# ConvFFN gate and up projections as one 2x2x2 Strassen block product on one Trainium2 core

## The chip, the cores and the metric

The kernel runs on one core of one Trainium2 chip. A core has TensorE (PE: matrix products out of SBUF into PSUM, with a weight load for each), VectorE (DVE), ScalarE (ACT), GpSimd (POOL) and SyncE (SP, whose queue issues the loads and stores). The metric is the device time of one execution in microseconds (us), the median of the runs.

## What is computed

One inference step of a one-layer hybrid decoder, D_MODEL 1024, 2048 prompt tokens and 8 x 4 sample tokens, all in fp32. The change touches the gated ConvFFN with D_FF = 3072, the last part of the layer:

```python
def causal_dwconv(x, prev, w, b):
    K = w.shape[0]
    T = x.shape[1]
    xp = jnp.concatenate([prev.astype(x.dtype), x], axis=1)
    y = b + sum(w[k] * xp[:, k:k + T] for k in range(K))
    return y, xp[:, T:]
...
    n3 = rmsnorm(x, p['g_ffn'])
    g, ffn_state = causal_dwconv(n3 @ p['w_ffn_gate'], ffn_prev, p['w_ffn_conv'], p['b_ffn_conv'])
    x = x + (jax.nn.gelu(g) * (n3 @ p['w_ffn_up'])) @ p['w_ffn_down']
    return x, (buf_k, buf_v, conv_state, h_last, ffn_state)
```

Ahead of it stand the input projection with a gated recurrence and windowed attention, the output projection and a cross-attention to 256 memory tokens; behind it the final RMSNorm.

## The kernel before

Channels and features lie on the 128 partitions, tokens along the free dimension. Each fp32 operand is split into a high and a low part (`split`, L75: ACT copies the high part at L78, DVE or POOL subtracts to get the low part at L82), and each product is three matmuls: high by high, high by low, low by high (`mm3`, L120).

The phases run in program order; a scheduler orders each engine's queue by priority and dependence, so phases overlap at their borders. Phases 0 to 2 take up to about 1100 us. Phase 3 is the ConvFFN. It takes the tokens in three blocks (SB3, L37: 704, 688, and 656 with the 32 sample tokens). For each block it reads the residual x back from DRAM (x2d), normalises it (`p3_norm`, L595) and keeps the split result n3 as 16 tiles, 8 channel tiles of 128 with a high and a low one each, out of 28 tile names that go round, so that 12 of a next block's tiles are others than this block's. The norm of block 0 is issued at a high priority (N3_PRIO), that of the next block after feature tile 20 of the 24; the scheduler puts those of its operations whose tiles are free much further ahead.

For each feature tile f of 128 (`gate_up`, L1149): the gate's and the up's 96 matmuls (8 channel tiles, 2 token halves, 3 products, 2 projections), into PSUM tiles named pg; ACT copies the gate to gb (L1166); DVE does the three convolution taps into gc (a tensor_scalar at L1176 and two scalar_tensor_tensor at L1178); ACT does the gelu (L1179); DVE multiplies with the up product, read out of PSUM (L1183); ACT and POOL split the result into ah and al. After every second f, `down` (L1197) does the 96 matmuls of the two f before it into PSUM tiles pd (8 output tiles), and DVE adds each to the accumulator acc (L1208). The product down(f-2, f-1) stands in the program behind gate_up(f), at a block's border behind the next block's first feature.

Weights come through `weights` (L107), in units of 128 x 1024 in the order of use, two units ahead: a DMA into wr (four buffers), the high part wh by ACT, the low part wl by POOL (three buffers each). A gate, an up or a down tile of a feature is one unit.

## Time and profile before

| | |
|---|---|
| median of 3 runs | 2786.28 us (2780.19 to 2796.98) |
| span of the profiled execution | 2790.0 us |
| busy over the span | PE 96%, DVE 50%, ACT 36%, POOL 44% |
| chain that ended last | PE 75%, DVE 3%, DMA 2%, POOL 1% |
| phase 3 | about 1100 us to the end |
| DMA | 276.91 MB, mean 99 GB/s |

Busy time counts an engine's instructions that compute; register, branch, semaphore and DMA-issuing ones are left out. The chain that ended last is followed back from the last instruction, at each step to what released it. Shares over the whole span mix phases with different limits, so phase 3 is read by itself in the rows below.

### The profile page before, as it was taken

What the parts mean: (1) busy time and instruction counts of PE and PEld (TensorE: products, weight loads), DVE (VectorE), ACT (ScalarE), POOL (GpSimd) and SP (SyncE); (2) the same over time, 40 slices, a digit from 0 to 9 for tenths busy, and PEclk for the clock granted to TensorE, in tenths of its full rate; (3) what the DMA queues carried; (4) which work ended last, traced back from release to release, by engine and by line L of the source; (5) the groups of instructions that cost most, each with busy time, mean ns of one, the idle gap of its engine ahead of it and who ended that gap; (6) DMA issues with size and microseconds to landing.
All of it is one profiled execution on the core that took longest, in us unless ns stands there. A gap on an engine that the chain in (4) does not pass through costs nothing.

```text
span 2790.0 us, 39744 instructions
## 1 busy us (share of the span) xinstructions
PE 2688.0 (96%) x16085; PEld 2531.3 (91%) x16085; DVE 1399.4 (50%) x2135; ACT 1011.5 (36%) x1749; POOL 1219.3 (44%) x802
## 2 busy tenths in 40 slices
PE   7998988998999998999999999999999999999997
PEld 6786867986998887999999999999999999999997
DVE  7568687758563545533333345333333443333435
ACT  5474736465453544322222223222222232222222
POOL 3444544314635364543434345444344454444343
PEclk8999999999999999999999999999999999999998
DMA  6342412244435344311121234212212241112121
GB/s 225 118 133 72 135 65 96 83 147 149 137 112 202 111 150 139 119 69 68 68 69 68 68 98 146 76 68 77 69 69 70 75 147 71 69 68 76 62 76 52
DMA packets 117463, 276.91 MB, mean 99 GB/s; under 512 B 19940, under 2 KB 40676, under 8 KB 117280
## 3 DMA queue, kind: packets, MB, share of 16 engines
q1 hardware_dynamic: 117280, 274.37, 28.9%
q8 instruction: 126, 2.06, 0.3%
q14 instruction: 57, 0.47, 0.1%
HBM read 244.13 MB, written 30.20 MB: 98 GB/s over the span
## 4 chain that ended last, share of the span: by engine, by line
PE 75%; DVE 3%; DMA 2%; POOL 1%; issue 1%; ACT 1%; SPq 0%; POOLq 0%; DVEq 0%; ACTq 0%
PE pg L125 37%; PE pd L125 19%; PE po L125 7%; PE pq L125 3%; PE pmo L125 3%; PE pin L125 2%; PE mpo L125 1%; DMA x<-x2d 1%; PE msc L125 1%; DMA yraw<-ymix 1%; PE mtp L1011 1%; DVE x L604 1%; PE spo L1127 0%; PE sst L1088 0%; PE pt L125 0%
## 5 line engine op out<-in xcount | busy, mean ns | idle before, releaser
L82 POOL TENSOR_TENSOR wl<-wr,wh 128x1024 fp32r<-128x1024 f32 x341 | 824.4, 2423 | 1313.0 <-ACT wh L78 1247.6
L125 PE MATMUL pg<-n,wh 128*128 128x344 f32 (+1 forms) x4608 | 919.0, 321 | 0.6 <-POOL n L82 0.3
L125 PEld LDWEIGHTS pg<-n,wh 128*128 128x128 f32 x4608 | 765.2, 188 | 1.2 <-POOL n L82 0.6
L78 ACT ACTIVATE wh<-wr 128x1024 fp32r<-128x1024 f32 x326 | 341.4, 1057 | 1100.7 <-PE pd L125 403.8
L125 PE MATMUL pg<-n,wl 128*128 128x344 f32 (+1 forms) x2304 | 552.1, 321 | 0.0
L1176 DVE TENSOR_SCALAR gc<-gb,pp 128x704 f32<-128x704 f32 (+1 forms) x72 | 146.7, 2037 | 542.2 <-ACT gb L1166 356.3
L125 PEld LDWEIGHTS pg<-n,wl 128*128 128x128 f32 x2304 | 398.9, 188 | 0.1
L1208 DVE TENSOR_TENSOR acc<-pd,acc 128x688 f32<-128x688 f32 (+1 forms) x280 | 246.4, 880 | 278.6 <-PE pd L125 273.5
L125 PE MATMUL pd<-ah,wh 128*128 128x344 f32 (+1 forms) x1120 | 270.5, 323 | 9.5 <-DVE acc L1208 9.5
L125 PE MATMUL pd<-al,wh 128*128 128x344 f32 (+1 forms) x1120 | 269.7, 322 | 0.0
L125 PE MATMUL pd<-ah,wl 128*128 128x344 f32 (+1 forms) x1120 | 269.5, 322 | 0.0
L125 PEld LDWEIGHTS pd<-ah,wh 128*128 128x128 f32 x1120 | 195.7, 190 | 10.4 <-DVE acc L1208 10.3
L125 PE MATMUL pin<-n1h,wh 128*128 128x512 f32 (+1 forms) x560 | 188.5, 361 | 9.4 <-DVE ql L82 9.4
L125 PEld LDWEIGHTS pd<-al,wh 128*128 128x128 f32 x1120 | 196.0, 190 | 0.0
L125 PEld LDWEIGHTS pd<-ah,wl 128*128 128x128 f32 x1120 | 195.6, 190 | 0.0
L125 PE MATMUL pin<-n1l,wh 128*128 128x512 f32 (+1 forms) x560 | 186.7, 358 | 2.1 <-DVE n1l L82 2.1
L125 PE MATMUL pin<-n1h,wl 128*128 128x512 f32 (+1 forms) x560 | 185.3, 356 | 0.0
L1179 ACT ACTIVATE gc<-gc 128x704 f32<-128x704 f32 (+1 forms) x72 | 56.8, 788 | 301.5 <-DVE gc L1178 301.5
L1178 DVE SCALAR_TENSOR_TENSOR gc<-gb,pp,gc 128x704 f32<-128x704 f32 (+1 forms) x144 | 141.9, 985 | 4.9
L125 PEld LDWEIGHTS pin<-n1h,wh 128*128 128x128 f32 x560 | 103.3, 193 | 25.8 <-DVE ql L82 9.7
L82 POOL TENSOR_TENSOR al<-at,ah 128x688 fp32r<-128x688 f32 (+1 forms) x72 | 124.1, 1724 | 5.7 <-ACT ah L78 5.7
L125 PEld LDWEIGHTS pin<-n1l,wh 128*128 128x128 f32 x560 | 102.8, 193 | 18.2 <-DVE n1l L82 4.1
(313 smaller groups left out, 3923.9 us busy)
## 6 DMA issues: line engine op xcount, KB each, us to landing
wr<-in_w_gate_dram SPq DMA_DIRECT2D x72, 512.0 KB, 3.2
wr<-in_w_up_dram SPq DMA_DIRECT2D x72, 512.0 KB, 3.2
wr<-in_w_down_dram SPq DMA_DIRECT2D x72, 512.0 KB, 3.2
wr<-in_w_in_dram SPq DMA_DIRECT2D x56, 512.0 KB, 3.2
...
wr<-in_w_out_dram SPq DMA_DIRECT2D x32, 512.0 KB, 3.3
...
wr<-in_w_mem_q_dram SPq DMA_DIRECT2D x16, 512.0 KB, 4.5
```

The lines of the kernel that those rows point to most:

```text
L78: nc.scalar.activation(hi, src, AF.Copy)
L82: e.tensor_tensor(out=lo, in0=src, in1=hi.bitcast(F), op=OP.subtract)
L125: nc.tensor.matmul(o, w[a], xs, start=first and n == 0, stop=last and n == 2)
L604: nc.vector.scalar_tensor_tensor(x, x, self.col(G_FFN, k), rt, op0=OP.mult, op1=OP.mult)
L1011: nc.tensor.transpose(tp[:, i], P[:, i, c * 128:(c + 1) * 128], K.ident)
L1176: nc.vector.tensor_scalar(gc, gb[:, 2:2 + NW], K.col(C_FW, 48 + f), K.col(C_FB, f), op0=OP.mult, op1=OP.add)
L1178: nc.vector.scalar_tensor_tensor(gc, gb[:, k:k + NW], K.col(C_FW, 24 * k + f), gc, op0=OP.mult, op1=OP.add)
L1179: nc.scalar.activation(gc, gc, AF.Gelu_apprx_tanh)
L1208: nc.vector.tensor_tensor(out=v, in0=pd[:, :, 0:H], in1=v, op=OP.add)
```

## The change

The gate and the up product of a feature tile are taken as one product of 2 x 2 blocks, A x B. A has the gate's first and second half of the channels (a11, a12) in its first row and the up's (a21, a22) in its second. B has the first and second half of the channels as rows and the two token halves of the block as columns (b11 to b22). Winograd's form of Strassen's product does this with seven block products and sums: of A, s1 = a21 + a22, s2 = s1 - a11, s3 = a11 - a21, s4 = a12 - s2; of B, t1 = b12 - b11, t2 = b22 - t1, t3 = b22 - b12, t4 = b21 - t2. ORDER and BUDDY list the pairs.

- Weights: `piece_stream` and `piece` take the place of `weights` in phase 3. Pieces are 128 x 512 (4 channel tiles), four ahead, six buffers for each of the high and low parts, three for sums, four raw buffers as before. DVE makes four sums `ws` per feature, ACT and POOL split seven pieces per feature and four per down product.
- Activations: `p3_norm` makes seven operands for each of four channel tiles, 28 pairs of high and low tiles of half a block's width, with four DVE subtractions for each; low parts alternate between POOL and DVE. The tiles n3_0 to n3_55 have one buffer each, and the next block's norm is issued after f = 23, no longer after 20. The x tiles have three buffers, and not two.
- Features: `gate_up` does 84 matmuls, accumulates in four PSUM halves X, Y, Z, V, and forms the two outputs by a copy u and adds u2, u4 and those into gb and up out of PSUM. The first convolution tap is done by ACT. up and gc have one buffer, and up x gc reads SBUF alone.
- Blocks are now 696, 692 and 660 with the 32 sample tokens.

```diff
-SB3 = [(0, 704, False), (704, 688, False), (1392, 656, True)]
+SB3 = [(0, 696, False), (696, 692, False), (1388, 660, True)]
+ORDER = ("a11", "s2", "s1", "s3", "a12", "s4", "a22")
+BUDDY = ("b11", "t2", "t1", "t3", "b21", "b22", "t4")
...
-            self.wspl = pool(name="wspl", bufs=3)
...
+    def piece_stream(self):
+
+        nc, I = self.nc, self.I
+
+        def load(src):
+            raw = self.wraw.tile([128, 1024], F, name="wr", tag="wr")
+            nc.sync.dma_start(raw, src)
+            return raw[:, 0:512], raw[:, 512:1024]
+
+        def sums(x, y, op):
+            t = self.wsum.tile([128, 512], F, name="ws", tag="ws")
+            nc.vector.tensor_tensor(out=t, in0=x, in1=y, op=op)
+            return t
+
+        def halves(src):
+            hi = self.wpc.tile([128, 512], R, name="ph", tag="ph")
+            lo = self.wpc.tile([128, 512], R, name="pl", tag="pl")
+            self.split(src, hi, lo, "act", "pool")
+            return hi, lo
+
+        def paired(f):
+            a11, a12 = load(I["w_gate"][f])
+            a21, a22 = load(I["w_up"][f])
+            yield halves(a11)
+            s1 = sums(a21, a22, OP.add)
+            s2 = sums(s1, a11, OP.subtract)
+            yield halves(s2)
+            yield halves(s1)
+            yield halves(sums(a11, a21, OP.subtract))
+            yield halves(a12)
+            yield halves(sums(a12, s2, OP.subtract))
+            yield halves(a22)
+
+        def plain(c):
+            raws = [load(I["w_down"][c * CH + i]) for i in range(CH)]
+            for h in range(2):
+                for i in range(CH):
+                    yield halves(raws[i][h])
+
+        for s in range(3):
+            for f in range(NF):
+                yield from paired(f)
+                if f % CH == 0 and (f or s):
+                    yield from plain((f // CH - 1) % (NF // CH))
+        yield from plain(NF // CH - 1)
...
+    def piece(self, ahead=4):
+        while len(self.pq) <= ahead:
+            p = next(self.pieces, None)
+            if p is None:
+                break
+            self.pq.append(p)
+        return self.pq.pop(0)
...
-                    if f == 20 and s < 2:
+                    if f == NF - 1 and s < 2:
...
-        x = self.xs.tile([128, W], F, name="x3", tag="x", bufs=2)
+        x = self.xs.tile([128, W], F, name="x3", tag="x", bufs=3)
...
-    def n3_tile(self, W):
-        i = self.n3i % 28
-        self.n3i += 1
-        return (self.n3a if i < 13 else self.n3b).tile([128, W], R, name=f"n3_{i}")
-
     def p3_norm(self, s):
         nc, q1 = self.nc, self.xs
         t0, w, smp = SB3[s]
         W = w + (NS if smp else 0)
+        H = W // 2
         rt = q1.tile([128, W], F, name="rt3")
         self.p3_dma(rt, self.r3d, t0, W)
-        nh, nl = [], []
-        for k in range(KT):
-            x = self.p3_load(s, k)
-            nc.vector.scalar_tensor_tensor(x, x, self.col(G_FFN, k), rt, op0=OP.mult, op1=OP.mult)
-            h, l = self.n3_tile(W), self.n3_tile(W)
-            self.split(x, h, l, "act", "pool" if k % 2 else "dve")
-            nh.append(h)
-            nl.append(l)
-        return nh, nl
+        ops, n = {}, 0
+        for k in range(KT // 2):
+            xs = []
+            for kk in (k, k + KT // 2):
+                x = self.p3_load(s, kk)
+                nc.vector.scalar_tensor_tensor(x, x, self.col(G_FFN, kk), rt, op0=OP.mult, op1=OP.mult)
+                xs.append(x)
+            b11, b12, b21, b22 = xs[0][:, 0:H], xs[0][:, H:W], xs[1][:, 0:H], xs[1][:, H:W]
+            v = dict(b11=b11, b21=b21, b22=b22)
+            for nm, x, y in (("t1", b12, b11), ("t2", b22, "t1"), ("t3", b22, b12), ("t4", b21, "t2")):
+                v[nm] = q1.tile([128, H], F, name="t3", tag="t", bufs=4)
+                nc.vector.tensor_tensor(out=v[nm], in0=x, in1=v[y] if isinstance(y, str) else y, op=OP.subtract)
+            for nm in BUDDY:
+                hl = []
+                for e in "hl":
+                    hl.append((self.n3a if n < 26 else self.n3b).tile([128, H], R, name=f"n3_{n}"))
+                    n += 1
+                self.split(v[nm], hl[0], hl[1], "act", "pool" if n % 4 else "dve")
+                ops[nm, k] = hl
+        return ops
...
-        K, nc, q1, q2, I, s = self.K, self.K.nc, self.K.q1, self.K.q2, self.K.I, self.s
-        w, W, H, NW, smp, subs = self.w, self.W, self.H, self.NW, self.smp, self.subs
-        res = []
-        for nm in ("w_gate", "w_up"):
-            wt = K.weights(I[nm][f])
-            ps = K.psum([128, 2, 512], "pg", "pg")
-            outs = [ps[:, e, 0:H] for e in range(2)]
-            K.proj(wt, self.nh, self.nl, outs, subs, KT)
-            res.append(ps)
-            if nm == "w_gate":
-                gb = q2.tile([128, NW + 2], F, name="gb")
-                if s == 0:
-                    nc.gpsimd.memset(gb[:, 0:2], 0.0)
...
-                    nc.gpsimd.tensor_copy(gb[:, 0:2], K.p3c[s - 1][:, f])
...
-                    nc.scalar.activation(gb[:, 2:2 + W].rearrange("p (a b) -> p a b", a=2), ps[:, :, 0:H], AF.Copy)
...
-                nc.gpsimd.tensor_copy(self.carry[:, f], gb[:, w:w + 2])
-                gc = q2.tile([128, NW], F, name="gc")
-                nc.vector.tensor_scalar(gc, gb[:, 2:2 + NW], K.col(C_FW, 48 + f), K.col(C_FB, f), op0=OP.mult, op1=OP.add)
-                for k in range(2):
-                    nc.vector.scalar_tensor_tensor(gc, gb[:, k:k + NW], K.col(C_FW, 24 * k + f), gc, op0=OP.mult, op1=OP.add)
-                nc.scalar.activation(gc, gc, AF.Gelu_apprx_tanh)
-        pu = res[1]
-        at = q1.tile([128, W], F, name="at", bufs=1)
-        if not smp:
-            nc.vector.tensor_tensor(out=at.rearrange("p (a b) -> p a b", a=2), in0=pu[:, :, 0:H],
...
+        K, nc, q1, q2, s = self.K, self.K.nc, self.K.q1, self.K.q2, self.s
+        w, W, H, NW, smp = self.w, self.W, self.H, self.NW, self.smp
+        xy = K.psum([128, 2, 512], "pg", "pg")
+        zw = K.psum([128, 2, 512], "pg", "pg")
+        X, Y, Z, V = (t[:, e, 0:H] for t in (xy, zw) for e in range(2))
+        add = lambda o, p, t: nc.vector.tensor_tensor(out=o, in0=p, in1=t, op=OP.add)
+        tmp = lambda nm: q2.tile([128, H], F, name=nm, tag="hv", bufs=3)
+
+        def product(i, out, first):
+            hi, lo = K.piece()
+            for k in range(KT // 2):
+                ws = [t[:, k * 128:(k + 1) * 128] for t in (hi, lo)]
+                K.mm3([out], ws, [[t] for t in self.ops[BUDDY[i], k]], first and k == 0, k == KT // 2 - 1, not first)
+
+        gb = q2.tile([128, NW + 2], F, name="gb")
+        if s == 0:
+            nc.gpsimd.memset(gb[:, 0:2], 0.0)
         else:
-            nc.vector.tensor_tensor(out=at[:, 0:H], in0=pu[:, 0, 0:H], in1=gc[:, 0:H], op=OP.mult)
...
+            nc.gpsimd.tensor_copy(gb[:, 0:2], K.p3c[s - 1][:, f])
+        up = q1.tile([128, W], F, name="up")
+        product(0, X, True)
+        u = tmp("u")
+        nc.scalar.activation(u, X, AF.Copy)
+        product(1, Y, True)
+        u2 = tmp("u2")
+        add(u2, Y, u)
+        product(2, Z, True)
+        u4 = tmp("u4")
+        add(u4, Z, u2)
+        product(3, V, True)
+        add(up[:, H:W], V, u4)
+        product(4, X, False)
+        nc.scalar.activation(gb[:, 2:2 + H], X, AF.Copy)
+        product(5, Z, False)
+        n = w - H
+        add(gb[:, 2 + H:2 + w], Z[:, 0:n], u2[:, 0:n])
+        if smp:
+            gv = gb[:, 2 + w:2 + w + 6 * NB].rearrange("p (b e) -> p b e", e=6)
+            nc.gpsimd.tensor_copy(gv[:, :, 0:2], K.fst[:, f])
+            bt = lambda t: t[:, n:H].rearrange("p (b t) -> p b t", t=NT)
+            add(gv[:, :, 2:6], bt(Z), bt(u2))
...
+        product(6, V, False)
+        add(up[:, 0:H], V, u2)
+        gc = q1.tile([128, NW], F, name="gc")
+        nc.scalar.activation(gc, gb[:, 2:2 + NW], AF.Identity, scale=K.col(C_FW, 48 + f), bias=K.col(C_FB, f))
+        for k in range(2):
+            nc.vector.scalar_tensor_tensor(gc, gb[:, k:k + NW], K.col(C_FW, 24 * k + f), gc, op0=OP.mult, op1=OP.add)
+        nc.scalar.activation(gc, gc, AF.Gelu_apprx_tanh)
+        nc.vector.tensor_tensor(out=up[:, 0:w], in0=up[:, 0:w], in1=gc[:, 0:w], op=OP.mult)
...
-        wts = [K.weights(K.I["w_down"][ch * CH + i]) for i in range(CH)]
         for m in range(KT):
+            if m % 4 == 0:
+                wts = [K.piece() for i in range(CH)]
             pd = K.psum([128, 2, 512], "pd", "pd")
             outs = [pd[:, e, 0:H] for e in range(2)]
             for i in range(CH):
-                ws = [t[:, m * 128:(m + 1) * 128] for t in wts[i]]
+                ws = [t[:, m % 4 * 128:(m % 4 + 1) * 128] for t in wts[i]]
```

Three places of DVE's queue show what stands where. First, block 0 in steady state. Before, the rows of a feature pair are two feature paths and the accumulator adds:

```order
L1176 TENSOR_SCALAR gc<-gb,pp 128x704
L1178 SCALAR_TENSOR_TENSOR gc<-gb,pp,gc 128x704 x2
L1183 TENSOR_TENSOR at<-pg,gc 128x704
L1176 TENSOR_SCALAR gc<-gb,pp 128x704
L1178 SCALAR_TENSOR_TENSOR gc<-gb,pp,gc 128x704 x2
L1183 TENSOR_TENSOR at<-pg,gc 128x704
L1208 TENSOR_TENSOR acc<-pd,acc 128x704 x8
```

Now, in the feature ahead of a down product (the u rows are the adds u2 and u4, ws are the weight sums, of the next feature from the first ws on):

```order
L1207 TENSOR_TENSOR u_13722<-pg,u 128x348
L1207 TENSOR_TENSOR u_13740<-pg,u_13722 128x348
L538 TENSOR_TENSOR ws<-wr 128x512
L538 TENSOR_TENSOR ws<-ws,wr 128x512
L538 TENSOR_TENSOR ws<-wr 128x512
L1207 TENSOR_TENSOR up<-pg,u_13740 128x348
L1207 TENSOR_TENSOR gb<-pg,u_13722 128x348
L1250 SCALAR_TENSOR_TENSOR gc<-gb,pp,gc 128x696 x2
L1207 TENSOR_TENSOR up<-pg,u_13722 128x348
L1274 TENSOR_TENSOR acc<-pd,acc 128x696
L1252 TENSOR_TENSOR up<-up,gc 128x696
L1274 TENSOR_TENSOR acc<-pd,acc 128x696 x2
```

Three of the next feature's four weight sums stand between the feature's add u4 and its add up, the fourth among the accumulator adds; the tap at L1176 is gone. Second, phase 2's end, of the cross-attention of the last tokens. Before, rows of block 0's norm (L604, L82) stood among its softmax:

```order
L996 SCALAR_TENSOR_TENSOR nm<-mx,rcs 128x2
L82 TENSOR_TENSOR ptl<-mtp,pth 128x512
L604 SCALAR_TENSOR_TENSOR x_10619<-x_10619,pp,rt_10568 128x704
L996 SCALAR_TENSOR_TENSOR nm<-mx,rcs 128x2
L82 TENSOR_TENSOR ptl<-mtp,pth 128x512
L604 SCALAR_TENSOR_TENSOR x_10627<-x_10627,pp,rt_10568 128x704
L1000 RECIPROCAL mrs<-mrs 128x4
L1002 TENSOR_SCALAR P<-P,mrs 128x256 x4
```

Now the norm (L647, L653) begins behind the last residual add of phase 2 (x_7, L1095):

```order
L1095 TENSOR_TENSOR x_7_9932<-pmo,x_7_9932 128x512
L538 TENSOR_TENSOR ws<-wr,ws 128x512
L538 TENSOR_TENSOR ws<-wr 128x512
L538 TENSOR_TENSOR ws<-ws,wr 128x512
L647 SCALAR_TENSOR_TENSOR x_10566<-x_10566,pp,rt_10563 128x696
L171 RECIPROCAL rc<-rc 128x4
L653 TENSOR_TENSOR t_10574<-x_10566 128x348
L647 SCALAR_TENSOR_TENSOR x_10570<-x_10570,pp,rt_10563 128x696
L188 COPY rt<-pr 128x512
L653 TENSOR_TENSOR t_10576<-x_10570,t_10574 128x348
```

All eight normalising products of block 0 moved behind phase 2's adds, with three weight sums ahead of them. Third, the border of blocks 0 and 1. Before, rows of block 2's norm (whose tiles came free with block 0's) stood there among down's adds:

```order
L82 TENSOR_TENSOR n_13_19202<-x_19196,n_12_19201 128x688
L1208 TENSOR_TENSOR acc<-pd,acc 128x704 x2
L604 SCALAR_TENSOR_TENSOR x_19214<-x_19214,pp,rt_19156 128x688
L1208 TENSOR_TENSOR acc<-pd,acc 128x704
L604 SCALAR_TENSOR_TENSOR x_19223<-x_19223,pp,rt_19156 128x688
L1208 TENSOR_TENSOR acc<-pd,acc 128x704 x4
L1176 TENSOR_SCALAR gc<-gb,pp 128x688
L1178 SCALAR_TENSOR_TENSOR gc<-gb,pp,gc 128x688 x2
L1183 TENSOR_TENSOR at<-pg,gc 128x688
L181 RECIPROCAL rc<-rc 128x5
```

Now, during feature 23 of block 0 (n are low parts of the next block's operands, t their differences, u, up and gb the feature's adds):

```order
L84 TENSOR_TENSOR n_7_15873<-t_15856,n_6_15872 128x346
L653 TENSOR_TENSOR t_15902<-x_15892,t_15898 128x346
L1207 TENSOR_TENSOR up<-pg,u_15750 128x348
L538 TENSOR_TENSOR ws<-wr,ws 128x512
L647 SCALAR_TENSOR_TENSOR x_15932<-x_15932,pp,rt_15841 128x692
L84 TENSOR_TENSOR n_11_15881<-x_15848,n_10_15880 128x346
L1207 TENSOR_TENSOR gb<-pg,u_15732 128x348
L653 TENSOR_TENSOR t_15940<-x_15932 128x346
L1250 SCALAR_TENSOR_TENSOR gc<-gb,pp,gc 128x696
L84 TENSOR_TENSOR n_27_15929<-t_15902,n_26_15928 128x346
L1207 TENSOR_TENSOR up<-pg,u_15732 128x348
```

The norm of block 1 stands in between the adds of feature 23 itself, and goes on behind them.

## Rows read from the trace of the kernel before

L is the line in the kernel before; `wr` is a raw weight, names are the program's tiles, out<-in.

**Rows 1.** The page's part 4: the chain that ended last, by line
```profile
PE pg L125 37%; PE pd L125 19%; PE po L125 7%; PE pq L125 3%; PE pmo L125 3%; PE pin L125 2%; PE mpo L125 1%; DMA x<-x2d 1%; PE msc L125 1%; DMA yraw<-ymix 1%; PE mtp L1011 1%; DVE x L604 1%; PE spo L1127 0%; PE sst L1088 0%; PE pt L125 0%
```

**Rows 2.** Busy us of each engine in 100 us of block 0
```profile
core 0: us, PE busy (x) PEld busy (x) DVE busy (x) ACT busy (x) POOL busy (x), PEclk, DMA share, GB/s
1400.00:1500.00 100.00, 100.00 (x621) 100.00 (x620) 37.19 (x36) 23.08 (x26) 37.99 (x25) 1.00 0.19 64
```

**Rows 3.** TensorE's waits, 1110 to 2700: us in total, times, longest
```profile
PE pd L125 <- DVE acc L1208: 9.5, 3, 5.2
```

**Rows 4.** The chain in order of time: start us, us, what
```profile
1173.68 31.04 PE pg L125 x192
...
2650.21 30.12 PE pg L125 x192
```

**Rows 5.** Groups of DVE, POOL, ACT by shape: xcount | busy, mean
```profile
L1208 DVE TENSOR_TENSOR acc<-pd,acc 128x688 f32<-128x688 f32 x184 | 160.9, 875 | 181.8 <-PE pd L125 176.7 <-DMA acc<-x2d 5.1
...
L1178 DVE SCALAR_TENSOR_TENSOR gc<-gb,pp,gc 128x704 f32<-128x704 f32 x96 | 94.2, 981 | 3.3
...
L1186 DVE TENSOR_TENSOR at<-pg,gc 128x344 f32<-128x344 f32 x24 | 12.4, 516 | 46.8 <-PE pg L125 45.8 <-ACT gc L1179 0.9
...
L1043 DVE TENSOR_TENSOR x<-pmo,x 128x512 f32<-128x512 f32 x8 | 5.4, 690 | 11.7 <-PE pmo L125 11.7
...
L1057 POOL TENSOR_TENSOR ssum<-ssum,sq 128x512 f32<-128x512 f32 x7 | 9.0, 1291 | 0.2
...
L82 POOL TENSOR_TENSOR al<-at,ah 128x688 fp32r<-128x688 f32 x48 | 81.0, 1688 | 5.7 <-ACT ah L78 5.7
...
L1049 ACT ACTIVATE sq<-x 128x512 f32<-128x512 f32 x10 | 6.3, 631 | 6.9 <-DVE x L1043 4.4 <-DVE x1s L1053 2.4
...
L1168 ACT ACTIVATE gb<-pg 128x344 f32<-128x344 f32 x24 | 10.5, 438 | 0.0
```

**Rows 6.** Timeline of DVE, then POOL: start us, us, engine, line
```profile
1653.08 0.86 DVE L82 TENSOR_TENSOR n<-x,n 128x688 fp32r<-128x688 f32 x1
...
1656.06 0.94 DVE L604 SCALAR_TENSOR_TENSOR x<-x,pp,rt 128x688 f32<-128x688 f32 x1 [1.26 <-DMA x<-x2d]
...
1657.78 2.22 DVE L604 SCALAR_TENSOR_TENSOR x<-x,pp,rt 128x688 f32<-128x688 f32 x1
1659.91 2.37 DVE L82 TENSOR_TENSOR n<-x,n 128x688 fp32r<-128x688 f32 x1
...
1656.65 2.61 POOL L82 TENSOR_TENSOR wl<-wr,wh 128x1024 fp32r<-128x1024 f32 x1 [1.53 <-DMA x<-x2d]
1659.22 2.33 POOL L82 TENSOR_TENSOR al<-at,ah 128x704 fp32r<-128x704 f32 x1
1661.52 2.31 POOL L82 TENSOR_TENSOR n<-x,n 128x688 fp32r<-128x688 f32 x1
```

**Rows 7.** The page's part 6, weight load: KB, us to landing
```profile
wr<-in_w_gate_dram SPq DMA_DIRECT2D x72, 512.0 KB, 3.2
```

**Rows 8.** Stretches around three TensorE waits; the matmuls that waited
```profile
1160.00:1166.00 6.00, 6.00 (x25) 6.00 (x24) 0.93 (x2) 0.00 (x0) 2.35 (x2) 0.57 0.26 87
1680.00:1685.00 5.00, 5.00 (x22) 5.00 (x22) 2.02 (x3) 1.58 (x2) 3.81 (x3) 0.61 0.33 84
1690.00:1695.00 5.00, 5.00 (x33) 5.00 (x32) 2.64 (x3) 3.44 (x5) 4.84 (x4) 1.00 0.00 0
...
1159.08 0.96 PE L125 MATMUL pd<-ah,wh 128*128 128x352 f32 x2 [3.49 <-DVE acc L1208]
...
1678.94 0.95 PE L125 MATMUL pd<-ah,wh 128*128 128x352 f32 x2 [5.22 <-DVE acc L1208]
...
1688.02 0.59 PE L125 MATMUL pd<-ah,wh 128*128 128x352 f32 x2 [0.76 <-DVE acc L1208]
```

**Rows 9.** Timeline of DVE, two rows ahead of the FFN
```profile
1060.89 0.95 DVE L604 SCALAR_TENSOR_TENSOR x<-x,pp,rt 128x704 f32<-128x704 f32 x1 [0.80 <-DMA x<-x2d]
...
1099.90 0.69 DVE L1043 TENSOR_TENSOR x<-pmo,x 128x512 f32<-128x512 f32 x1 [2.07 <-PE pmo L125]
```

More of the change, by code (lines that the diff above doesn't have):

```diff
@@ L118, in weights, with mm3 @@
         return self.wq.pop(0)
-    def mm3(self, outs, w, x, first, last):
+    def mm3(self, outs, w, x, first, last, more=False):
         nc = self.nc
@@ L124, in mm3 @@
             for o, xs in zip(outs, x[b]):
-                nc.tensor.matmul(o, w[a], xs, start=first and n == 0, stop=last and n == 2)
+                nc.tensor.matmul(o, w[a], xs, start=first and n == 0, stop=last and n == 2, skip_group_check=more)
     def proj(self, w, xh, xl, outs, subs, nk):
@@ L562, in phase3 @@
                     if len(pend) == CH:
[L563 removed]
+                        (sb if f else last).down(pend)
                         pend = []
@@ L1220, in tail @@
         nc.sync.dma_start(K.O["s_ffn_conv"], K.sfo)
-        wts = [K.weights(K.I["w_down"][NF - CH + i]) for i in range(CH)]
+        wts = [K.piece() for i in range(2 * CH)]
         warm = K.q2.tile([128, 1], F, name="warm")
```

62 lines of the change are left out of this document (23 added, 39 removed).

## The prediction

> **What bounds the kernel now.** I began with the chain that ended last [rows 1]: the FFN's two products on TensorE (PE), pg (gate and up) and pd (down), carry 37 and 19% of the span in it. Then a stretch of the FFN phase, which runs from about 1100 us to the end [rows 2]: in steady state PE is busy all of 100 us at full granted clock, DVE 37%, POOL 38%. The list of PE's waits says the same from the other side [rows 3]: from 1110 to 2700 us pd waited three times, 9.5 us in all. So a matmul removed there is time removed, if the new feeding work keeps up. The chain in order of time prices the matmuls [rows 4]: 192 of 352 columns take 31.04 us (161.7 ns each), 192 of 344 take 30.12 (156.9). One pair of features (2 f and the down product after them, 288 matmuls) costs 46.56 or 45.17 us, by the three blocks 45.6 in the mean (288 x 161.7 or 156.9).
>
> **What is removed.** Seven block products of 4 x 3 matmuls take the place of eight, so a feature needs 84 matmuls and not 96: 72 x 12 = 864 fewer. The new halves of 348, 346 and 346 columns lie between the two priced sizes, 158.5 ns in the mean. Removed: 864 x 0.1585 = **-137 us**, and a pair without a wait would take 264 x 0.1585 = 41.8 us. The order of instructions does have these counts, so "it does not do what it says" is no case here.
>
> By the Trainium skill, "TensorE: Matmul & The Clock Gate", section "Back-to-back issue gap", a warm matmul takes its columns over 2.4 GHz plus about 2.5 ns, an estimate of 147.5 ns at 348 columns and so 127 us removed. The rows here are 14 ns above that rate at 352 and 344 columns, and the sum goes by the rows.
>
> **What is added in every pair of features.** DVE gets eight weight sums `ws` of 512 columns, adds of half width out of PSUM (u2, u4, two up, one gb) in each feature, and a product up x gc that now has both inputs in SBUF; its first tap goes to ACT. POOL makes eighteen low parts of 512 columns in place of six of 1024 columns. Durations [rows 5]: low part 1.29 (a POOL operation of the same kind and size), `al` 1.69, sum about 0.69 (a 512-column add), half-width add 0.52, tap 0.98, up x gc about 0.88 (between 0.86 and 0.94 of [rows 6]), ACT's high part of 512 columns 0.63, half-width copy 0.44.
>
> PE no longer has a cheap supply. Two things decide: how the supply loop is closed, and what DVE and POOL do to each other.
>
> *DVE against POOL.* [rows 6] shows the same kinds of operation together. DVE's normalising product, 0.94 us at 1656.06, took 2.22 at 1657.78, when it came while POOL made a low part; it ended at 1660.00, 0.78 behind POOL's end. POOL's next one, 1.69 in the mean [rows 5], took 2.33; DVE's next subtraction, 0.86 at 1653.08, took 2.37; POOL's next took 2.31. They pass each other in turn, one whole instruction each. The accumulator adds with one input in PSUM do not take part: 875 ns in the mean of 184, though POOL is busy 38% of the time [rows 2, 5]. So `ws`, the taps and up x gc take turns with POOL and the adds from PSUM don't. Demand on that turn per pair: POOL 18 x 1.29 + 2 x 1.69 = 26.6, DVE 8 x 0.69 + 4 x 0.98 + 2 x 0.88 = 11.2, together 37.8 of 41.8 us. It would just fit if it could be spread at will.
>
> The Trainium skill, "SBUF — State Buffer", section "Who interferes with whom", gives this as a rule against such a change: a DVE instruction with two SBUF inputs and a GpSimd instruction that reads SBUF exclude each other, and the later one waits out the whole of the first. The rows agree (2.22 us for 0.94). If the rule were soft, and the two shared, the case "no turns" below would be the forecast.
>
> *The loop.* Call B the feature ahead of a down product, C the next one. The raw weights have four buffers, so the load of C's up weights waits until the low part of B's seventh piece is made; that piece needs the buffer of B's first piece, which frees when PE ends product 1 of B. In DVE's queue the three sums of C that need this load stand ahead of the add up[H:] of B, and PE's sixth product of B waits for that add, since it writes the same PSUM tile. From the end of product 1 of B: copy u 0.44, high part 0.63, low part 1.29 (ended at 2.43 with what the hops take, some 0.03 each), issue to landing 3.2 [rows 7] with another hop: landed at 5.70. POOL meanwhile goes on with `al` (to 4.12), D0 (5.41), D1 (6.70). The first sum, 0.29 us too late for D1, runs 6.70 to 7.39; D2 to 8.68, second sum to 9.37, D3 to 10.66, third to 11.35, add to 11.87. PE has four products until then, 48 x 0.1585 = 7.6 us. It waits **4.3 us**; if the first sum slips in ahead of D1, **3.0**; if nobody takes turns, 5.70 + 3 x 0.69 + 0.52 = 8.3, **0.7**. I take 3.0: the margin is 0.29 us, and anything that holds POOL back puts the sum first.
>
> *The clock.* The two long gaps of before tell what such a wait brings after it [rows 8]. After 3.49 us the granted clock was 0.57 in 1160 to 1166, and 25 matmuls ran in 6 us, where 5 us hold 33 at clock 1.00 (1690 to 1695): 2.2 us lost. After 5.22 us it was 0.61 in 1680 to 1685, 22 in place of 33: 1.7 us lost. That is mostly the lower of its two levels, 1.2 GHz. After the wait of 0.76 us at 1688 it stood at 1.00. So 3.0 us of waiting costs 5.0. The other waits of a pair (the fourth sum stands ahead of the gb add in the feature without a down product; PE's next product reads a PSUM tile that ACT still copies) come to 0.6, at most 1.2.
>
> Stall per pair 3.0 + 2.0 + 0.6 = **5.6 us** (1.3 without turns, 7.7 with the late sum). Steady pairs are 36 less one at the start of each block: 33 x 5.6 = **+185 us** (43 to 254). A pair then lasts 47.4 us against 45.6.
>
> **Start of the FFN.** Before, block 0's eight normalising products ran inside phase 2 (the last at 1060.89), and PE could go from phase 2's products to pg [rows 9]; counted back from 1173.68 [rows 4] by the 384 matmuls done, 384 x 0.1617, it started in effect at 1111.6. Now all of block 0's operands come behind phase 2's last add (1099.90 + 0.69): 8 x 0.94 + 16 x 0.52 + 14 x 0.52 = 23 us on DVE, 14 x 0.92 (the line through POOL's 512 and 688 columns in [rows 5]) = 13 on POOL. In turn that is 36, to about 1136, and product 1 needs the last channel tile of it: **+24 us**. If DVE's 23 alone count, +12; with waits for the three x buffers, +40.
>
> **Two block seams.** Before, most of a next block's norm ran a block ahead, into tiles that were partly doubled; the losses were the 6 us of [rows 3] that came behind the 3.49. Now all operands are single, so they can be overwritten only while feature 23 runs its products, and down(22,23) stands behind the next block's first feature. Norm (18 on DVE, 13 on POOL) and the weight pieces (16 us) make about 47 us in turn over 13.3 us of PE work: a gap of 34; with DVE and POOL side by side 13. I take 27 each, 54 less 6 us that seams cost before: **+48** (20 to 62).
>
> **Sum.** -137 + 185 + 24 + 48 = +120 on the profiled 2790.0 us: 2910. The median of the runs is 3.7 us below the span, so 2906.
>
> **Rivals.**
> - *PE stays the bound* (faster). The four pieces of lead absorb the loop, because a hand schedule puts waits in line that a queue hides. Stall under 1 us a pair: -137 + 30 + 12 + 20 = -75, **2711 us**. For it: PE's share of [rows 2], and the turn's demand of 37.8 is under 41.8. Against: lead in pieces does not move the load, which hangs on the buffer of product 1. It decides if PE's stall stays under 2 us a pair, for (137 - 24 - 48)/33 = 2.0 is the point of no gain or loss.
> - *No turns*, the load alone late: 33 x 1.3 = 43: -137 + 43 + 24 + 48 = -22, **2764**. Against it are the two DVE rows over 2 us of [rows 6].
> - *Late sum each time*: 254 in place of 185, **2975**; it belongs to the forecast's side.
>
> **Chances.** Forecast with the late sum 0.70, PE bound 0.17, no turns 0.13. A measurement of this kernel tells about 0.5% (14 us) from no change. The first gives 0.68 slower and 0.02 same; the second is faster; the third, with its start and seams free, 0.05 faster, 0.05 same, 0.03 slower. Faster 0.22, same 0.07, slower 0.71. The range leaves out a tenth at each end: 2700 (a little below PE bound) to 2985 (late sum, with part of the worse seams).
>
> **What will show it.** Matmuls of the FFN fall by 864. Right: PE's waits list pg behind DVE's up, ws or POOL's low parts, once a pair and over 2.5 us; `ws` means well above 0.69 us; granted clock of a steady 100 us below 0.97; a pair every 47 to 50 us; gaps of 20 us or more at the start and the two seams. Wrong: a pair of 42 to 43.5 us at clock 1.00 (PE bound), or long PE waits with `ws` at 0.7 (no turns). If the pairs are right and the start is not, the last x reloads are the term to look at.

## The result, and the profile after

The changed kernel takes 2981.14 us (median of 4 runs, 2978.46 to 2989.74), the kernel before 2786.98 beside it (4 runs, 2780.19 to 2796.98): 1.070 times as long, 95% interval 1.067 to 1.073. That is on the side that was forecast and inside its range (2700 to 2985), though by 4 us only, and 75 us above the 2906 forecast. The profiled execution's span is 2980.4 us, 190.4 more than before.

The page's first part, of the changed kernel: busy time, share of the span, instructions.

```profile
PE 2669.9 (90%) x15221; PEld 2438.5 (82%) x15221; DVE 1829.8 (61%) x2789; ACT 1279.3 (43%) x2337; POOL 1616.3 (54%) x1264
```

PE has the 864 matmuls fewer (16085 before), and is busy 90% of a longer span, where it was 96%. The same 100 us as in [rows 2], and 4 us behind one of its waits, with the same columns:

```profile
1400.00:1500.00 100.00, 91.50 (x545) 87.44 (x545) 53.16 (x65) 36.01 (x59) 57.69 (x49) 0.98 0.21 68
...
1424.00:1428.00 4.00, 3.71 (x14) 3.71 (x15) 0.30 (x2) 0.17 (x1) 0.94 (x1) 0.57 0.83 255
```

PE is busy 91.5 us where it was 100, and DVE and POOL are only half busy: no engine is full. What PE waits for, over the whole span (the view of [rows 3]):

```profile
PE pg L121 <- DVE up L1207: 79.1, 62, 2.6
PE pd L121 <- DVE acc L1274: 57.3, 36, 3.2
PE pg L121 <- ACT n L80: 21.0, 6, 4.4
...
PE pg L121 <- DVE n L84: 13.9, 3, 6.2
```

The first two come mostly from the steady pairs, the two of n from the norm at the start and the seams. One pair in the timeline (start us, us, engine, line, and in brackets the idle time before with its releaser), PE first, then DVE, then POOL:

```profile
1421.83 0.32 PE L121 MATMUL pg<-n,pl 128*128 128x348 f32 x1
1424.29 0.95 PE L121 MATMUL pg<-n,ph 128*128 128x348 f32 x2 [2.14 <-DVE up L1207]
...
1420.02 1.33 DVE L538 TENSOR_TENSOR ws<-wr 128x512 f32<-128x512 f32 x1 [1.21 <-DMA wr<-in_w_up_dram]
1421.44 0.69 DVE L538 TENSOR_TENSOR ws<-ws,wr 128x512 f32<-128x512 f32 x1
1422.05 1.76 DVE L538 TENSOR_TENSOR ws<-wr 128x512 f32<-128x512 f32 x1
1423.73 0.51 DVE L1207 TENSOR_TENSOR up<-pg,u 128x348 f32<-128x348 f32 x1
...
1438.40 1.75 DVE L538 TENSOR_TENSOR ws<-wr,ws 128x512 f32<-128x512 f32 x1 [1.85 <-POOL pl L84]
1440.07 0.87 DVE L1274 TENSOR_TENSOR acc<-pd,acc 128x696 f32<-128x696 f32 x1
...
1418.25 2.55 POOL L84 TENSOR_TENSOR pl<-wr,ph 128x512 fp32r<-128x512 f32 x2
1421.70 3.24 POOL L84 TENSOR_TENSOR pl<-wr,ph 128x512 fp32r<-128x512 f32 x2 [0.90 <-ACT ph L80]
```

The forecast loop is there. DVE stands idle until the up weights land at about 1420.0; its first sum takes 1.33 us beside POOL's low part, the second, while POOL waits for ACT, 0.69, the third 1.76. Only then comes the add that PE waits for: 2.14 us listed as idle. The second wait was not in the forecast. The fourth sum waits 1.85 us for one of POOL's low parts, because the sums have three buffers, and then takes 1.75; behind it in DVE's queue stands the accumulator add at 1440.07, on which the down product waits. The groups of 1250 to 1600 us by shape (count | busy us, mean ns | idle before) answer to [rows 5]:

```profile
L538 DVE TENSOR_TENSOR ws<-wr 128x512 f32<-128x512 f32 x29 | 32.1, 1108 | 17.7 <-POOL pl L84 9.5 <-DMA wr<-in_w_up_dram 8.2
...
L538 DVE TENSOR_TENSOR ws<-wr,ws 128x512 f32<-128x512 f32 x14 | 24.6, 1759 | 22.8 <-POOL pl L84 22.8
...
L1207 DVE TENSOR_TENSOR up<-pg,u 128x348 f32<-128x348 f32 x28 | 14.4, 513 | 16.2 <-PE pg L121 16.2
```

Sums of two raw halves last 1.1 us in the mean and the fourth sum 1.76, where a 512-column add had taken 0.69; the second sum, which in block 0 meets POOL waiting for ACT, keeps 0.69; adds out of PSUM stay at 0.51. From the end of one down product to the next, 28 steady pairs took 1366.5 us (10 from 1204.18 to 1690.94, 9 from 1869.69, 9 from 2487.47): 48.8 us a pair, 7.0 above the 41.84 of its matmuls.

### The profile page after: what moved, and what is told of

Same layout as the page of the kernel before. It is cut to its first block, busy times and chain, and to the rows that moved or that the text cites. A ratio compares the mean times of both kernels' runs of the same rounds, so it can differ in the third digit from the quotient of the medians.

```text
span 2980.4 us, 41018 instructions
## 1 busy us (share of the span) xinstructions
PE 2669.9 (90%) x15221; PEld 2438.5 (82%) x15221; DVE 1829.8 (61%) x2789; ACT 1279.3 (43%) x2337; POOL 1616.3 (54%) x1264
## 5 line engine op out<-in xcount | busy, mean ns | idle before, releaser
L121 PE MATMUL pg<-n,ph 128*128 128x346 f32 (+1 forms) x4032 | 1012.4, 337 | 145.6 <-DVE up L1207 79.1
L121 PEld LDWEIGHTS pg<-n,ph 128*128 128x128 f32 x4032 | 712.7, 195 | 206.5 <-DVE up L1207 99.0
L84 POOL TENSOR_TENSOR pl<-wr,ph 128x512 fp32r<-128x512 f32 x360 | 500.1, 1399 | 451.9 <-ACT ph L80 430.6
L121 PE MATMUL pg<-n,pl 128*128 128x346 f32 (+1 forms) x2016 | 647.6, 329 | 1.0 <-POOL pl L84 1.0
L84 POOL TENSOR_TENSOR wl<-wr,wh 128x1024 fp32r<-128x1024 f32 x125 | 306.4, 2453 | 550.0 <-ACT wh L80 454.9
L84 POOL TENSOR_TENSOR pl<-ws,ph 128x512 fp32r<-128x512 f32 x288 | 379.8, 1329 | 177.6 <-ACT ph L80 177.4
L121 PEld LDWEIGHTS pg<-n,pl 128*128 128x128 f32 x2016 | 392.8, 196 | 1.4 <-POOL pl L84 1.3
L121 PE MATMUL pd<-ah,ph 128*128 128x346 f32 (+1 forms) x1120 | 282.4, 331 | 62.0 <-DVE acc L1274 57.3
L121 PE MATMUL pd<-ah,pl 128*128 128x346 f32 (+1 forms) x1120 | 276.8, 325 | 2.4 <-POOL pl L84 2.4
L121 PE MATMUL pd<-al,ph 128*128 128x346 f32 (+1 forms) x1120 | 274.9, 327 | 2.4 <-POOL al L84 2.4
```

What stands on the lines that cost most here:

```text
L84: e.tensor_tensor(out=lo, in0=src, in1=hi.bitcast(F), op=OP.subtract)
L121: nc.tensor.matmul(o, w[a], xs, start=first and n == 0, stop=last and n == 2, skip_group_check=more)
```

## The experiments

Each line of edit is against the changed kernel, unless another is named; lines left out are marked by dots. The kernel before took 2787 to 2793 us beside all of them. Every variant but the last was run once, and the four runs of the changed kernel lie 11 us apart, so differences of some 12 us in the whole say little by themselves.

### Does it need both partners of the turn?

All low parts of weights on DVE, which leaves POOL `al` and small copies in the steady pairs:

```diff
-            self.split(src, hi, lo, "act", "pool")
+            self.split(src, hi, lo, "act", "dve")
```

> All low parts of weight pieces are made by DVE, none by POOL, which keeps those of al and of the norm. DVE's work in a pair grows by 18 x 0.69 = 12.4 to about 36 of 41.8 us, all in one queue. Turn theory: with POOL out of the way each sum takes 0.69 us and each low part 0.69 in place of 1.29 to 1.4, waits on up and acc fall under 1 us a pair: pair 43 to 44, the whole about 2981 - 33 x 5 = 2810. Loop theory: the loop gets 0.6 us shorter for the low part and 1.8 for the turns, so that up waits are nearly gone, but the buffer of sums still holds the accumulator adds: pair about 45.5, 2870. Rival: DVE in order becomes the late engine, its low parts stand ahead of the adds that TensorE needs, pair 48 or more, no gain.

And, with POOL as it was, no sums, so that the kernel leaves out part of the product:

```diff
-            t = self.wsum.tile([128, 512], F, name="ws", tag="ws")
-            nc.vector.tensor_tensor(out=t, in0=x, in1=y, op=op)
-            return t
+            return x
```

> The weight sums are left out: pieces take a raw half in the place of each sum, so the output is not the reference's; matmuls, splits, loads and adds are all as before. If the pair's 7 us above the matmuls come from the sums (their place ahead of the adds, their turns with POOL, their buffer), a pair falls to 42 to 43 us and the whole by 33 x 6 = 200 us to about 2780, with start and seams left as they are. If the matmuls or the PSUM adds are themselves slower in this form, the pair stays above 46 us and the whole above 2900.

Measured: 2794.78 and 2798.33 us, each within 20 of what was expected; a steady pair takes 43.7 and 43.5 in the mean. With the low parts on DVE, its sums of 1250 to 1600 us by shape:

```profile
L538 DVE TENSOR_TENSOR ws<-wr 128x512 f32<-128x512 f32 x32 | 21.9, 684 | 1.8 <-DMA wr<-in_w_up_dram 1.6
```

PE's waits in the same 350 us:

```profile
PE pg L121 <- DVE up L1207: 1.4, 8, 0.2
```

and the window of [rows 2]:

```profile
1400.00:1500.00 100.00, 99.61 (x609) 96.17 (x608) 77.17 (x116) 38.80 (x62) 10.02 (x12) 1.00 0.22 73
```

Without sums, the same window:

```profile
1400.00:1500.00 100.00, 99.51 (x613) 97.03 (x613) 41.19 (x55) 38.75 (x62) 62.94 (x53) 1.00 0.20 64
```

PE's waits of 1250 to 1600 us:

```profile
PE pg L121 <- DVE up L1205: 2.0, 8, 0.3
```

and POOL's low parts there:

```profile
L84 POOL TENSOR_TENSOR pl<-wr,ph 128x512 fp32r<-128x512 f32 x146 | 188.0, 1302 | 108.8 <-ACT ph L80 107.8 <-DVE gc L1248 1.0
```

In the first DVE has more work than ever, 77%, and PE loses next to nothing (99.61 us busy of 100); in the second POOL makes all its low parts at 1.30 us each. Neither the work of the sums nor that of POOL costs time by itself. The two together cost some 185 us (2981.14 less 2794.78 or 2798.33). Neither run alone tells the turns from the sums' place in DVE's queue: the second takes the sums away, and in the first only two of a feature's first three sums still stand ahead of the add up[H:] (at 1428.42 and 1429.14 us in DVE's timeline, the add at 1430.25), the third behind it. By the changed kernel's own rows, though, the turns are most of the first wait: the three sums there take 1.33 + 0.69 + 1.76 = 3.78 us, where three of 0.69 would take 2.07, and PE waits 2.14. The Trainium skill, "SBUF — State Buffer", section "Who interferes with whom", says that a DVE instruction with two SBUF inputs and a GpSimd one that reads SBUF exclude each other. The runs agree with it: sums of two raw halves take 0.684 us without POOL's low parts, and 1.108 with them.

### Is it the raw buffer, or the sum buffers?

A fifth raw buffer, for the second down tile of a pair, so that the up weights load earlier:

```diff
-        def load(src):
-            raw = self.wraw.tile([128, 1024], F, name="wr", tag="wr")
+        def load(src, own=False):
+            raw = (self.wrd if own else self.wraw).tile([128, 1024], F, name="wrd" if own else "wr", tag="wrd" if own else "wr")
...
-            raws = [load(I["w_down"][c * CH + i]) for i in range(CH)]
+            raws = [load(I["w_down"][c * CH + i], i == CH - 1) for i in range(CH)]
...
+            self.wrd = pool("wrd", 1)
```

> The second down tile of each pair is loaded into a buffer of its own, so that the load of the next feature's up weights no longer waits for the low part of the seventh piece, but for that of the fifth. Nothing else is changed. Loop theory (the raw buffer closes the loop, the late sums hold the add up that TensorE waits for): TensorE's waits on up, 2.1 us a pair, and the half-clock stretches behind them vanish, a pair falls from 48.8 to about 46 us, the whole by 33 x 2.8 = some 90 us to about 2890. Turn theory (the sums are late because DVE and POOL take turns, wherever the load lands): the sums still last 1.1 to 1.8 us each and stand ahead of the add, waits on up stay above 1.5 us a pair, the whole within 20 us of 2981.

Measured: 2969.27 us, 12 less, as the turn theory had it. PE's waits of 1250 to 1600 us, seven pairs of block 0:

```profile
PE pg L121 <- DVE u L1208: 22.3, 7, 3.2
...
PE pg L121 <- DVE up L1208: 1.1, 7, 0.2
```

The timeline of DVE and then POOL in one of the pairs:

```profile
1473.51 1.80 DVE L538 TENSOR_TENSOR ws<-wr 128x512 f32<-128x512 f32 x1
1475.40 2.00 DVE L538 TENSOR_TENSOR ws<-ws,wr 128x512 f32<-128x512 f32 x1
1477.32 1.74 DVE L538 TENSOR_TENSOR ws<-wr 128x512 f32<-128x512 f32 x1
1478.98 1.13 DVE L1208 TENSOR_TENSOR u<-pg,u 128x348 f32<-128x348 f32 x2
...
1473.46 1.30 POOL L84 TENSOR_TENSOR pl<-wr,ph 128x512 fp32r<-128x512 f32 x1 [0.57 <-ACT ph L80]
1474.71 2.13 POOL L84 TENSOR_TENSOR al<-up,ah 128x696 fp32r<-128x696 f32 x1
1476.80 1.71 POOL L84 TENSOR_TENSOR pl<-wr,ph 128x512 fp32r<-128x512 f32 x1
1478.47 1.72 POOL L84 TENSOR_TENSOR pl<-wrd,ph 128x512 fp32r<-128x512 f32 x1
```

The late load is gone, and the wait is not: with the weights there, the scheduler puts the three sums ahead of u2, they go in strict turns with POOL, and PE waits 3.2 us on u2. But the three blocks differ. A steady pair of block 0 takes 50.1 us in the mean (48.7 in the changed kernel), of block 1 48.5 (48.5), of block 2 46.5 (49.2). PE's first wait in block 2, 2520 to 2920 us, eight pairs:

```profile
PE pg L121 <- DVE u L1208: 2.5, 7, 0.4
```

There the three sums fall where POOL waits for PE ahead of its `al` and meet hardly any of its work (in one pair 0.69, 0.68 and 0.68 us at 2655.62, 2658.19 and 2658.79 in DVE's timeline), and the first wait is nearly gone, as the loop theory had it. So the loop through the raw buffer, which the prediction made the first of its two causes, does carry the first wait where the freed sums find POOL mostly idle (block 2); where they meet its low parts, the buffer sets which add is late, not that one is.

Five sum buffers in place of three, to take away the wait of the fourth sum:

```diff
-            self.wsum = pool("wsum", 3)
+            self.wsum = pool("wsum", 5)
```

> Five buffers for the weight sums, not three. The fourth sum of a feature then need not wait until the low part of its first sum is made, and no longer holds the accumulator adds behind it. If the waits of the down product (1.54 us a pair, 1.8 with their restart) and of gb (0.4) are made by that buffer, they vanish and the whole falls by 33 x 2.2 = 70 us to about 2910, with the waits on up left. If they come from DVE being late in any case, they stay and the time is within 15 us of 2981.

Measured: 2991.85 us, 11 more: the second expectation. The fourth sum in 1250 to 1600 us:

```profile
L538 DVE TENSOR_TENSOR ws<-wr,ws 128x512 f32<-128x512 f32 x15 | 14.7, 979 | 0.0
```

PE's waits there:

```profile
PE pg L121 <- DVE up L1207: 16.7, 14, 2.2
PE pd L121 <- DVE acc L1274: 9.8, 8, 1.2
```

The fourth sum no longer waits (0.0 idle) and runs 0.98 us in place of 1.76; a steady pair takes 47.7 us in the mean of block 0, but 51.6 in block 2. There, from 2520 to 2920 us, PE's longest wait in total is

```profile
PE pg L121 <- DVE up L1207: 35.1, 16, 4.3
```

In block 0 the fourth sum stands behind the add up[H:] (1425.89 us, behind 1425.46); in block 2 it stands ahead of it, as the last of four sums of 1.56 to 1.75 us in turn with POOL (2703.46 to 2709.98, the add at 2709.98). The buffer more let the scheduler move it there. So this edit takes away the wait that it aims at, and the time is lost in another.

### Fewer turns

The sums on POOL itself:

```diff
-            nc.vector.tensor_tensor(out=t, in0=x, in1=y, op=op)
+            nc.gpsimd.tensor_tensor(out=t, in0=x, in1=y, op=op)
```

> The weight sums are made by POOL and not by DVE; low parts stay on POOL. Nothing of DVE's queue stands ahead of TensorE's adds any more, as in the run without the sums, but POOL now has 26 low parts and sums of 1.29 us and two al in a pair, 37 of 41.8 us, and the taps and up x gc of DVE (5.7 us) take turns with it. If what cost was only the place of the sums in DVE's queue, a pair is 43 to 44 us and the whole about 2800. If the room of the turn counts (37 + 5.7 = 43 us a pair, POOL the late engine), a pair is 46 to 49 and the whole 2900 to 2990, with TensorE waiting for POOL's pl.

Measured: 2914.1 us, in the range of the second expectation, with a pair of 45 to 47.5, but PE waits for the add up and not for POOL's pl. Of 1250 to 1600 us, DVE's taps and its adds up:

```profile
L1250 DVE SCALAR_TENSOR_TENSOR gc<-gb,pp,gc 128x696 f32<-128x696 f32 x30 | 53.4, 1781 | 17.1 <-ACT gc L1248 16.6
...
L1207 DVE TENSOR_TENSOR up<-pg,u 128x348 f32<-128x348 f32 x30 | 15.4, 513 | 35.6 <-PE pg L121 30.2 <-POOL ws L538 5.4
```

PE's longest wait in total there:

```profile
PE pg L121 <- DVE up L1207: 17.0, 8, 2.1
```

Now the taps are the ones that wait for turns, 1.78 us for the 0.96 they took in the changed kernel. POOL is busy 85% of 1400 to 1500, and 5.4 us of the idle time ahead of the add up end with POOL's sums. Other DVE instructions meet POOL's now, and 119 of the 186 us stay (2914.1 - 2794.78).

Low parts of the sums on DVE, those of raw halves on POOL:

```diff
-        def halves(src):
+        def halves(src, e="pool"):
...
-            self.split(src, hi, lo, "act", "pool")
+            self.split(src, hi, lo, "act", e)
...
-            yield halves(s2)
-            yield halves(s1)
-            yield halves(sums(a11, a21, OP.subtract))
+            yield halves(s2, "dve")
+            yield halves(s1, "dve")
+            yield halves(sums(a11, a21, OP.subtract), "dve")
...
-            yield halves(sums(a12, s2, OP.subtract))
+            yield halves(sums(a12, s2, OP.subtract), "dve")
```

> Only the eight low parts of sums in a pair are made by DVE, the ten of raw halves stay on POOL. The demand on the turn is then POOL 10 x 1.29 + 2 x 1.69 = 16.3 and DVE 16 x 0.69 + 3.9 + 1.8 = 16.7 us, 33 in place of 37.8 (all on POOL) and 27 (all on DVE). If what the pair loses goes with the turns, it lies between the two, 44.5 to 46.5 us, the whole 2830 to 2900, and sums last between 0.69 and 1.3 us where POOL works on a raw half. If only the place of a POOL low part ahead of a sum in the chain counts, which is gone here too for the sums' own parts, the pair is that of the run with all on DVE, 43.5, and the whole within 15 us of 2795.

Measured: 2894.72 us, a pair of 46.6 in the mean: the first expectation, at its upper end. The sums of raw halves and the fourth sum in the same stretch:

```profile
L538 DVE TENSOR_TENSOR ws<-wr 128x512 f32<-128x512 f32 x30 | 34.2, 1141 | 10.0 <-DMA wr<-in_w_up_dram 9.8
...
L538 DVE TENSOR_TENSOR ws<-wr,ws 128x512 f32<-128x512 f32 x15 | 10.3, 689 | 0.3
```

The only wait of PE there:

```profile
PE pg L121 <- DVE up L1207: 18.6, 16, 2.1
```

The second wait goes wholly (there is no pd behind acc, and the fourth sum is back at 0.69), the first stays (18.6 us, 16.0 in this stretch of the changed kernel; the sums of raw halves still take 1.14). So the two waits are separate, and half of POOL's low parts keep 100 of the 186 us (2894.72 - 2794.78).

### The seams

From the kernel with all low parts on DVE, the norm of blocks 1 and 2 left out (a second edit, in `mm3`'s operands, only cuts block 0's tiles to the block's half width):

```diff
-                        self.n3[s + 1] = self.p3_norm(s + 1)
+                        self.n3[s + 1] = self.n3[0]
```

> As the run with DVE's low parts (2794.8), and the norm of blocks 1 and 2 is left out: they use block 0's operands, so the output is not the reference's. What falls is the price of the two seams' norm. The seams there hold 40 and 38 us above their matmuls, of which about 2 x 5 are the ordinary waits of their three pairs. If the norm makes the rest, the whole falls by 55 to 65 us to about 2735; if the seam's cost is the final norm and the load of the accumulators at that place, by less than 25.

and, with the norm, the last down product of a block ahead of the next block's first feature:

```diff
-                if f % CH == 0 and (f or s):
-                    yield from plain((f // CH - 1) % (NF // CH))
-        yield from plain(NF // CH - 1)
+                if f % CH == 0 and f:
+                    yield from plain(f // CH - 1)
+            yield from plain(NF // CH - 1)
...
+                        sb.down(pend)
+                        pend = []
```

> As the run with DVE's low parts, and at a seam the block's last down product stands ahead of the next block's first feature, so that TensorE has 15 us of work while the norm runs. If the seam is a hole because no matmul is ready, each seam gets up to 15 us shorter less the 5 us until al of feature 23 is there: the whole falls by 15 to 25 us to about 2775. If DVE is what is late at the seam (norm, low parts and adds in one queue), the accumulator adds lengthen its queue and nothing is won: 2790 to 2800.

Measured: 2753.57, 41 less than with the norm, so 20 a seam, between the two expectations; and 2789.5, 5 less, the second one. That such 5 us are more than noise, the whole does not show; in the traces each seam is about 5 us shorter, and the start 3 longer. Three pairs at the first seam, 125.5 us of matmuls, take 165.8 us with the norm and 144.1 without. In the middle of that seam, 1640 to 1660 us, with all low parts on DVE:

```profile
1640.00:1660.00 20.00, 9.28 (x44) 7.17 (x43) 20.00 (x26) 10.18 (x20) 11.62 (x10) 0.78 0.32 98
```

and with the earlier down product too:

```profile
1640.00:1660.00 20.00, 15.08 (x78) 13.39 (x79) 20.00 (x26) 10.36 (x21) 13.15 (x11) 0.89 0.36 106
```

DVE is busy all of 20.00 us in both. The down product fills PE here, 15.08 us for 9.28, but DVE is the late one, and a seam gains only half of the 10 us that the first expectation had at most. The 18.5 us that a seam loses without a norm were not traced further.

### A version that beats both

Low parts on DVE and the earlier down product, and besides the low parts of the norm on DVE and its t tiles in a pool of their own (the order of the pools changes with it), so that the norm can begin earlier:

```diff
-                v[nm] = q1.tile([128, H], F, name="t3", tag="t", bufs=4)
+                v[nm] = self.tp.tile([128, H], F, name="t3", tag="t", bufs=4)
...
-                self.split(v[nm], hl[0], hl[1], "act", "pool" if n % 4 else "dve")
+                self.split(v[nm], hl[0], hl[1], "act", "dve")
```

> DVE's low parts, the flush at the seam, the norm's low parts all on DVE too, and the small tiles of the norm (t) moved from the right side of SBUF to a pool of their own: the right side then no longer reaches into phase 2's last tiles, and three normalising products of block 0 can run inside phase 2. If DVE with POOL's turns is what makes the start (about 22 us) and the seams (about 35 each) long, it falls by 10 at the start and 2 x 15 at the seams, to about 2755. If the norm is bound by its loads and tiles and not by DVE, 2780 or more.

and on top of that `al` on DVE too:

```diff
-        K.split(up, ah, al, "act", "pool")
+        K.split(up, ah, al, "act", "dve")
```

> As the run with all of DVE's low parts, flush and layout (2784.6), and the low part al of the activations on DVE too, so that POOL has no work that takes turns with DVE in phase 3 but the final norm's. Per pair 2 x 0.88 us more on DVE (39 of 43.4), and al is there 0.8 us sooner, also at the flush, where TensorE waited 5.3 us for it. If that wait counts, 2 x 3 to 5 us at the seams: about 2776, level with or just under the kernel before. If DVE's queue is full there, 2785 to 2795.

Measured: 2784.61, and 2779.89 (median of 10 runs, 2775.82 to 2785.76) against 2792.66 of the kernel before (13 runs, 2783.47 to 2798.09): 0.9963, interval 0.9948 to 0.9977. That is faster than the changed kernel by far, and than the kernel before by 0.4%, clear of the noise of these runs. The first of the two met its second expectation, and the second lies between its own two; that `al` on DVE helps is not shown, for the single 2784.61 lies within the range of the ten runs. The pair stays at 43.6. The longest single wait left with `al` on DVE stands in the seam, here in PE's timeline:

```profile
1658.40 0.66 PE L121 MATMUL pg<-n,pl 128*128 128x346 f32 x1 [8.81 <-DVE pl L84]
```

In the first of the two the start did not move: its first down product ends at 1192.7 us, 1190.2 with the low parts on DVE alone. Phase 2's last residual add, though, came at 1099.33 in place of 1094.06, so from there on it is 3 us shorter. What bounds the norm now, its work or its loads, was not separated.

## Why the prediction was right, and where it was off

| term, us | forecast | measured |
|---|---|---|
| removed (864 x 0.1585) | -137 | -137 |
| 28 steady pairs | 28 x 5.6 = +157 | 1366.5 - 28 x 41.84 = +195 |
| start | +24 | 1148.7 - 1111.6 = +37 |
| two seams, with 4 more pairs | 54 + 4 x 5.6 = +76 | 178.75 + 180.9 - 6 x 41.84 = +109 |
| losses of before in the FFN | -6 | -16 |
| tail, with the last pair | +6 | +2 |
| sum | +120 | +190 (span: +190.4) |

*What was removed* was priced by rows at 352 and 344 columns; now that 348 are to be seen, a down product starts two matmuls every 0.32 us (1432.60, 1432.92, 1433.24 in PE's timeline), 0.159 each. By the Trainium skill, "TensorE: Matmul & The Clock Gate", section "Back-to-back issue gap", it would be an estimate of 0.1475, by the page's formula for an isolated gap; the rows are longer, and decide. The prediction's own comparison has a slip: its rows are 12.5 and 11.1 ns above that rate, not 14, which changes no term.

*The mechanism* was right in its main part: 864 matmuls go, and turns between DVE's two-input SBUF instructions and POOL take more than that back. The two runs that remove one partner show that it takes both, and the lengths of the sums that it goes by turns; the rivals "PE stays the bound" (a pair of 42 to 43.5 at clock 1.00) and "no turns" are what those runs look like, not the changed kernel. The signs named ahead are there, two of them a little off: one long wait on up a pair (2.1 us, not over 2.5), `ws` of 1.1 to 1.76 us, a clock of 0.98 and not below 0.97 in 100 us, a pair of 48.8, in 47 to 50. The turns fall on the sums: the taps, which I had counted with them, keep 0.96 us, and up x gc takes 0.96 for 0.88. The other half of the mechanism, the loop through the raw buffer, is needed only in part: without it block 2's pairs fall to 46.5 us, and those of blocks 0 and 1 do not fall.

*The stall of a pair* was put at 5.6 and is 7.0, by other parts than I gave. In block 0 it is 6.6 (48.68 in the mean, less 264 x 0.1593 = 42.06 of matmuls), and start-to-start times give: up 2.4 (3.0 forecast); acc 1.8 (none forecast); gb 0.7 and the second up 0.4 (0.6 together); clock 0.8 (2.0); 0.5 in delays of 0.1 at the head of a product. So that the sum comes near is in part luck: a clock term too high by 1.2 stands against a wait of 1.8 that was not forecast. The failed step is "the loop": it followed only the first three sums and stopped at PE's sixth product. The fourth I had put ahead of the gb add alone; in DVE's queue it also stands ahead of accumulator adds. That the first wait was shorter than 3.0 is since the second sum met POOL waiting for ACT, and did not have to give way.

*The clock term* was mis-sized. [rows 8] had waits of 3.49 and 5.22 us; those of 2.1 us bring the lower level (0.57 in 1424 to 1428, after 2.14) only in a part of the pairs; what decides in which was not settled. Five of block 0's ten pairs take 47.9 to 48.0 us and five 49.4, which leaves 48.7 - 47.9 = 0.8 in the mean.

*The start* is 37, by the effective start of the matmuls: 348 were done at 1204.18, so 1204.18 - 348 x 0.1593 = 1148.7, against 1111.6. The norm went as forecast: on DVE it ran from 1103.13 to 1137.50, in turn with POOL, 34 us for 36. What was missing comes behind it, in DVE's timeline:

```profile
1137.43 1.94 DVE L647 SCALAR_TENSOR_TENSOR x<-x,pp,rt 128x692 f32<-128x692 f32 x1
1139.29 0.51 DVE L1207 TENSOR_TENSOR u<-pg,u 128x348 f32<-128x348 f32 x1
...
1147.39 1.76 DVE L538 TENSOR_TENSOR ws<-wr,ws 128x512 f32<-128x512 f32 x1 [1.18 <-POOL pl L84]
...
1150.74 0.51 DVE L1207 TENSOR_TENSOR gb<-pg,u 128x348 f32<-128x348 f32 x1
```

A normalising product of the next block (692 columns) stands ahead of the add u, and PE waits 2.33 us; two late sums stand ahead of gb, 2.83 us; and the granted clock of 1132 to 1148 is 0.73. I had taken PE to run freely once the norm was done. And the 37 hide something: phase 2's last residual add began at 1092.45, 7.5 us sooner than before (1099.90). Counted from there, the FFN's start costs some 45 us. That phase 2 gains by the norm's leaving it is near at hand, but was not tested.

*The seams* cost 109 in place of 76. Of 109, the ordinary stall of two pairs at each (28) leaves about 40 us for a seam's own, where 27 were forecast between 13 (side by side) and 34 (in turn): above both. That bound held the norm as one gap. PE's waits in the first seam, 1690 to 1870 us:

```profile
PE pg L121 <- DVE n L84: 6.2, 1, 6.2
PE pg L121 <- DVE up L1207: 5.5, 3, 2.3
PE pd L121 <- DVE acc L1274: 5.5, 4, 3.2
PE pg L121 <- DVE u L1207: 4.8, 5, 2.1
```

The window of the seam, with the columns of [rows 2]:

```profile
1691.00:1870.00 179.00, 147.81 (x819) 138.23 (x818) 129.03 (x147) 74.22 (x125) 121.75 (x94) 0.92 0.33 103
```

Waits on the operands n are a part only; u, up and acc wait too, since DVE also feeds the features that run meanwhile, and the clock is 0.92 in the mean of all three pairs. What the norm's share is was measured only with the low parts on DVE, where the seams stand 40 and 38 us above their matmuls and leaving out the norm saved 41: about half.

*Before's own losses* were 16 us and not 6: its FFN took 2770.67 - 1111.6 = 1659.1 us, its matmuls 1643.3. I had counted two listed waits, not the time.

*Why the change gains so little even without turns.* Of 137 us removed, a pair keeps 1.6 us back (43.5 in most of them, against 41.84: some ten delays of 0.06 to 0.34 us mostly at the head of products, whose cause was not tested), 28 x 1.6 = 46; a start of 22 and seams of 35 to 40 each take the rest. In the kernel before, with its 12 spare tiles, all such losses of the FFN came to 16.
